# The opening of a transformer layer on one core: weight splits, second-half statistics and small vectors put in another order

## The chip, the cores and the metric

The kernel runs on one core of a Trainium2 chip. A core has TensorE (PE, matmuls), VectorE (DVE), ScalarE (ACT), GpSimd (POOL) and SyncE (SP, which here only issues DMAs), each with its own queue worked off in order, an on-chip memory of 128 partitions (SBUF) and accumulation banks (PSUM), and 16 DMA engines to HBM. The metric is the device time of one execution in microseconds (us); the number to predict is the median after the change.

## The reference

One encoder layer over 1024 tokens of width 1024: an input LayerNorm, one projection, three attention groups, an output projection, a second LayerNorm, a squared-ReLU feed-forward of width 4096 and a third LayerNorm.

```python
x = layer_norm(x, ln_in_g, ln_in_b)
proj = x @ w_in[l]
qa, ka, va, qb, kb, vb, qc, kc, vc = jnp.split(proj, split_points, axis=-1)
oa = neighbourhood_attention(...)      # 8x16 windows on a 16x64 grid, 4 heads
ob = sliding_window_gqa(...)           # +-128 tokens, sink logit per head, 8 heads
oc = differential_attention(...)       # p1 - lam * p2, 4 heads, RMS norm per head
mix = jnp.concatenate([oa, ob, oc], axis=-1) @ w_out[l]
x = layer_norm(alpha * x + mix, ln_mix_g[l], ln_mix_b[l])
hdn = jax.nn.relu(x @ w_ff1[l])
x = layer_norm(alpha * x + (hdn * hdn) @ w_ff2[l], ln_ff_g[l], ln_ff_b[l])
```

In the differential attention `lam = exp(sum(lq0*lk0)) - exp(sum(lq1*lk1)) + 0.2`, and the normed output is scaled by `diff_subln_g * 0.8`.

## The kernel before

Every float32 operand of a matmul is split into a high part (rounded to the type fp32r that TensorE takes) and a low part (the rest), and each product is three matmuls: high by high, high by low, low by high (`mm3`, line 138). A weight block is split by a cast and a subtraction.

The opening goes like this. Four token tiles of 128x1024 are loaded (`load_x(range(4))`, line 180), then constants, the first weights of the queries and keys of the differential attention (`first_w`, line 333, called for QC and KC), the other four tiles, the value weights (`load_vc`, line 373) and the norm's rows. `ln_half` (line 223) does four tiles at a time: `ln_stats` on VectorE (L208 statistics, L215 aggregate, L217 add epsilon), a power on GpSimd (L218), then the normalisation in place, on ScalarE (L234) or, for the second and fourth tile of the first half, on VectorE (L228). Then for each of eight feature blocks four PE transposes into one PSUM bank (L239), an eviction with gain and offset on ScalarE (L241), the cast to the high part on VectorE or ScalarE (L246, L244) and the subtraction for the low part on VectorE (L247). The transposes of the first tile run over the five banks that are free, then those of the second tile, and so on, so a bank is complete when the fourth tile is.

`first_w` casts the weight on VectorE (L338) and subtracts on GpSimd (L339). `feat_pieces` (line 342) does 24 matmuls for a half (`mm_feat`, line 328) and evicts them. `t5_vectors` (line 271) makes the relative-bias vectors with a few matmuls, `split_vc` (line 379) casts the value weights on ScalarE and subtracts on VectorE (L130 through `sub`), `vc(t)` does 24 matmuls of 256 columns for one token tile. `ln_rows_out` (line 253) writes the scaled norm as rows to HBM: two products with alpha and, for each tile, a product and a sum on GpSimd (L260), in place, so behind the tile's transposes. `scalars` (line 308) loads the lambda, sink and sub-norm vectors through SP's queue and works on them with small instructions; its place is behind the second half's features.

The order of the instructions on each engine is not the program's: with `schedule_with_timeline_sim` a planner sets it before the run, from its own estimates of times, with the program's order as priority. `tc.issue_after(ins)` adds for the instructions in its block an edge of order behind `ins`, for those on the engine of `ins` alone, with no semaphore. The 36 buffers of `page` hold tiles, features and weights.

## Time and profile before

| | |
|---|---|
| median of 3 runs | 1190.77 us (1190.58 to 1192.29) |
| profiled execution, its own time | 1192.13 us |
| its span from first to last instruction | 1190.4 us, mean granted TensorE clock 0.99 |
| busy, PE / VectorE / ScalarE / GpSimd | 1141.3 / 953.1 / 642.1 / 414.6 us |
| the chain that ended last | PE 79% of the span, VectorE 5%, ScalarE 3% |

The engines' busy shares are means over stages: projections and attention up to about 600 us, the feed-forward behind it. L12 is line 12 of the kernel before. In a timeline a line is one instruction or several of one kind (x2), with its start, its length, what it writes and reads, and in brackets the engine's idle time ahead of it with what ended that. Matmuls overlap, so the distance from one start to the next is what one costs.

### The profile page before, as it was taken

To read this page: it belongs to the slowest core of one execution; us is meant where nothing else is said; L and a number is where in the kernel's file an instruction comes from. 1 tells how busy PE (TensorE), PEld (TensorE's weight loads), DVE (VectorE), ACT (ScalarE), POOL (GpSimd) and SP (SyncE) were. 2 spreads that over 40 slices of the span, in tenths; PEclk is the share of its full clock that TensorE was granted. 3 is DMA by queue.
4 is the path that set the end of the run, shared out by engine and by line. 5 is a ranking of instruction groups with operands and counts; after the bars stand their busy time and mean duration, and the time that the engine had idled before them with its cause. 6 is when DMAs were issued, how large, how long until landed. Compare 5 with 4: busy or idle time off the path is not lost.

```text
span 1190.4 us, 17144 instructions
## 1 busy us (share of the span) xinstructions
PE 1141.3 (96%) x5642; PEld 947.8 (80%) x5642; DVE 953.1 (80%) x1858; ACT 642.1 (54%) x1253; POOL 414.6 (35%) x368
## 2 busy tenths in 40 slices
PE   3999999999998989998999999999999999999996
PEld 2788889878877878876788888888888888888885
DVE  7566899998656688976779998999774988787985
ACT  4435666666556887765664544445553444444530
POOL 3875666685665775430121222222210000000201
PEclk9999999999989989999999999999999999999998
DMA  8566845362878971214376687766599754355731
GB/s 278 154 237 207 263 143 172 113 171 89 264 212 239 223 168 54 89 71 125 117 237 211 226 277 264 258 246 233 185 333 348 225 197 163 115 164 181 232 122 71
DMA packets 139408, 228.46 MB, mean 192 GB/s; under 512 B 11884, under 2 KB 76300, under 8 KB 139320
## 3 DMA queue, kind: packets, MB, share of 16 engines
q1 hardware_dynamic: 123800, 178.60, 47.7%
q0 software_dynamic: 15520, 48.77, 11.9%
q8 instruction: 45, 0.74, 0.3%
q14 instruction: 43, 0.35, 0.1%
HBM read 157.54 MB, written 77.60 MB: 198 GB/s over the span
## 4 chain that ended last, share of the span: by engine, by line
PE 79%; DVE 5%; ACT 3%; issue 2%; POOL 0%; DMA 0%; SPq 0%; DVEq 0%; ACTq 0%; POOLq 0%
PE psm L144 15%; PE psS L967 11%; PE psS L1097 11%; PE pst L967 7%; PE psm L967 7%; PE pst L1097 5%; PE psm L1097 5%; PE pspv L1097 4%; PE pspv L515 2%; PE psS L471 2%; PE pst L500 2%; PE pspv L754 1%; DVE pg L130 1%; PE pspv L652 1%; PE psS L725 1%
## 5 line engine op out<-in xcount | busy, mean ns | idle before, releaser
L144 PE MATMUL psm<-pg,whi 128*128 128x512 f32 x448 | 153.5, 408 | 2.1 <-DVE pg L246 1.8
L218 POOL TENSOR_TENSOR bnve<-bnve,pw 128x1 f32<-128x1 f32 x24 | 22.5, 940 | 360.7 <-DVE bnve L217 357.5
L1097 PE MATMUL psS<-pg,pg 128*128 128x512 f32 x576 | 140.5, 389 | 0.0
L967 PE MATMUL psS<-pg,pg 128*128 128x512 f32 x576 | 136.2, 393 | 2.4 <-ACT pg L827 2.4
L967 PEld LDWEIGHTS psS<-pg,pg 128*128 128x128 f32 x576 | 108.6, 189 | 25.2 <-ACT pg L827 2.9
L1097 PEld LDWEIGHTS psS<-pg,pg 128*128 128x128 f32 x576 | 108.1, 188 | 22.4
L827 ACT CAST pg<-hr 128x512 fp32r<-128x512 f32 x112 | 69.3, 619 | 95.3 <-PE pst L1097 40.8
L144 PEld LDWEIGHTS psm<-pg,whi 128*128 128x128 f32 x448 | 84.2, 192 | 22.0 <-DVE pg L246 2.2
L478 ACT ACTIVATE pg<-pg,cst 128x1024 f32<-128x1024 f32 x64 | 73.9, 1154 | 51.4 <-DVE cst L474 48.4
L144 PE MATMUL psm<-pg,wlo 128*128 128x512 f32 x224 | 89.7, 401 | 0.8 <-POOL wlo L161 0.8
L967 PE MATMUL psm<-pg,pg 128*128 128x512 f32 x384 | 89.8, 389 | 0.0
L967 PE MATMUL pst<-pg,pg 128*128 128x512 f32 x384 | 89.6, 389 | 0.0
L828 DVE TENSOR_TENSOR pg<-hr,pg 128x512 fp32r<-128x512 f32 x112 | 76.7, 685 | 13.0 <-ACT pg L827 12.9
L967 PEld LDWEIGHTS psm<-pg,pg 128*128 128x128 f32 x384 | 72.1, 188 | 15.0
L967 PEld LDWEIGHTS pst<-pg,pg 128*128 128x128 f32 x384 | 72.1, 188 | 15.0
L130 DVE TENSOR_TENSOR pg<-pst,pg 128x512 fp32r<-128x512 f32 (+2 forms) x112 | 64.9, 589 | 22.6 <-ACT pg L640 8.4
L485 POOL TENSOR_TENSOR pg<-pg,cst 128x704 f32<-128x704 f32 x32 | 49.2, 1537 | 80.1 <-DVE cst L482 52.7
L1097 PE MATMUL pst<-pg,pg 128*128 128x512 f32 x288 | 74.2, 389 | 0.0
L1097 PE MATMUL psm<-pg,pg 128*128 128x512 f32 x288 | 74.2, 389 | 0.0
L975 POOL DMA_DIRECT2D hd<-evb x80 | 43.2, 541 | 86.4 <-DVE evb L823 82.0
L144 PE MATMUL psm<-whi,pg 128*128 128x256 f32 (+1 forms) x256 | 71.5, 346 | 0.8 <-DVE pg L130 0.5
L827 ACT CAST pg<-evb 128x512 fp32r<-128x512 f32 x80 | 48.6, 617 | 39.5 <-DVE evb L823 39.4
(208 smaller groups left out, 2758.8 us busy)
## 6 DMA issues: line engine op xcount, KB each, us to landing
hr<-hd SPq DMA_DIRECT2D x28, 1024.0 KB, 5.7
hd<-evb POOLq DMA_DIRECT2D x80, 256.0 KB, 3.8
w1r<-in_w_ff SPq DMA_DIRECT2D x16, 1024.0 KB
evb<-in_w_ff SPq DMA_DIRECT2D x64, 256.0 KB, 3.7
qk<-evb SPq DMA_DIRECT2D x52, 256.0 KB, 3.9
y<-pg POOLq DMA_DIRECT2D x24, 512.0 KB, 4.4
pg<-y SPq DMA_DIRECT2D x24, 512.0 KB, 5.5
pg<-in_w_ff SPq DMA_DIRECT2D x32, 256.0 KB, 7.8
```

What stands on the lines that cost most here:

```text
L130: nc.vector.tensor_tensor(out=o, in0=a, in1=b, op=ALU.subtract)
L144: mm = nc.tensor.matmul(o, a, b, start=(i == 0), stop=(i == n - 1))
L471: last_mm[0] = nc.tensor.matmul(sc, q[:, m, (i % 2) * P:(i % 2) * P + P], kst[h][kh][:, m, :], start=True, stop=True)
L478: nc.scalar.activation(out=rt, in_=rt, func=AF.Exp, scale=-1.0, bias=sm[:, m:m + 1], accum_out=sm[:, 2 + m:3 + m])
L485: nc.gpsimd.tensor_tensor(out=R[1][:, a], in0=R[1][:, a], in1=sm[:, 6:7].broadcast_to([P, C_POOL]), op=ALU.mult)
L500: nc.tensor.transpose(pt[:, kb * P:(kb + 1) * P], src[:, c0:c0 + P], ident)
L515: nc.tensor.matmul(pv[:, 0:256], Vc[h // 2][kb // 4][:, kb % 4, h % 2, :], src[:, kb % 4, :], start=(n == 0), stop=(n == 15))
L827: nc.scalar.copy(out=pg[:, 0], in_=x)
L828: last_split[0] = nc.vector.tensor_tensor(out=pg[:, 1], in0=x, in1=f32(pg[:, 0]), op=ALU.subtract)
L967: nc.tensor.matmul(o, w[:, e, k], xo[m][k][:, f], start=(n == 0), stop=(n == 11))
L975: nc.gpsimd.dma_start(out=hd_d[m - 1, j], in_=x)
L1097: nc.tensor.matmul(o, h[:, e, sl], w[:, f], start=(k == 0 and n == 0), stop=(k == 15 and n == 2))
```

## The change

Seven edits, all in the opening:

- `first_w` falls into `first_load` and `first_split`. The casts of the first two weights go behind the last VectorE normalisation of the first half (`last_norm`), their subtractions on GpSimd behind that half's last power (`last_pow`).
- `ln_half` falls into `ln_norm` and `ln_feats`. The second half's statistics on VectorE go behind the subtraction of the first half's seventh feature (`dc < 7` instead of `dc < 5`); before, only the normalisation had such a rule, of no effect on ScalarE.
- With these first weights `mm_feat` does the 16 products of the high weights first, then the eight of the low ones.
- `split_vc` subtracts on GpSimd instead of VectorE, behind the first weights' subtractions, and comes ahead of `t5_vectors`.
- The rows on GpSimd come behind these subtractions (`last_pool`).
- The small vectors are loaded by five DMAs from ScalarE's queue ahead of all others of the opening; `scalars` comes behind the first half's last VectorE normalisation, the difference for lambda goes to GpSimd behind the value weights and its offset to ScalarE (`lam_sum`).
- The value weights are loaded ahead of the second four token tiles.

```diff
--- before.py
+++ after.py
@@ -178,6 +178,36 @@
             xs.append(x_t)
     load_x(range(4))
+    lq = const([P, 2, 32], "lq")
+    lk = const([P, 2, 32], "lk")
+    lam = const([P, 4], "lam")
+    neglam = lam[:, 3:4]
+    g08 = const([P, 1], "g08")
+    sink = const([P, 8], "sink")
+    negsink = const([P, 8], "negsink")
+    nc.scalar.dma_start(out=lq, in_=bcast_row(A["diff_lam_q"], 64))
+    nc.scalar.dma_start(out=lk, in_=bcast_row(A["diff_lam_k"], 64))
+    for j in range(2):
+        nc.scalar.dma_start(out=g08[64 * j:64 * j + 64, :], in_=A["diff_subln_g"])
+    nc.scalar.dma_start(out=sink, in_=bcast_row(A["sw_sink"], 8))
+    def scalars():
+        nc.vector.tensor_tensor(out=lq, in0=lq, in1=lk, op=ALU.mult)
+        nc.vector.tensor_reduce(out=lam[:, 0:2], in_=lq, op=ALU.add, axis=AX.X)
+        nc.scalar.activation(out=lam[:, 0:2], in_=lam[:, 0:2], func=AF.Exp)
+        nc.vector.tensor_scalar(out=g08, in0=g08, scalar1=1.0 - LAM_INIT, scalar2=None, op0=ALU.mult)
+        nc.vector.tensor_scalar(out=negsink, in0=sink, scalar1=-1.0, scalar2=None, op0=ALU.mult)
+    def lam_sum():
+        with tc.issue_after(last_pool[0].ins):
+            nc.gpsimd.tensor_tensor(out=lam[:, 2:3], in0=lam[:, 1:2], in1=lam[:, 0:1], op=ALU.subtract)
+        nc.scalar.activation(out=lam[:, 3:4], in_=lam[:, 2:3], func=AF.Identity, bias=lam0)
+    lam0 = const([P, 1], "lam0")
+    nc.vector.memset(lam0, -LAM_INIT)
     ident = const([P, P], "ident")
     load(out=ident, in_=A["c_ident"])
     pw = const([P, 16], "pw")
@@ -220,18 +250,21 @@
     last_sub = [None]
-    def ln_half(xs, half, cols):
+    def ln_norm(xs, half):
         for j in range(4):
-            mean, rstd = ln_stats(xs[j])
+            with (tc.issue_after(last_sub[0].ins) if half else ExitStack()):
+                mean, rstd = ln_stats(xs[j])
             if half == 0 and j % 2:
-                nc.vector.tensor_scalar(out=xs[j], in0=xs[j], scalar1=mean, scalar2=rstd,
-                                        op0=ALU.subtract, op1=ALU.mult)
+                last_norm[0] = nc.vector.tensor_scalar(out=xs[j], in0=xs[j], scalar1=mean, scalar2=rstd,
+                                                       op0=ALU.subtract, op1=ALU.mult)
                 continue
             nmr = small([P, 1], "nmr", 2)
             nc.vector.scalar_tensor_tensor(out=nmr, in0=mean, scalar=-1.0, in1=rstd, op0=ALU.mult, op1=ALU.mult)
-            with (tc.issue_after(last_sub[0].ins) if half else ExitStack()):
-                nc.scalar.activation(out=xs[j], in_=xs[j], func=AF.Identity, scale=rstd, bias=nmr)
+            nc.scalar.activation(out=xs[j], in_=xs[j], func=AF.Identity, scale=rstd, bias=nmr)
+    def ln_feats(xs, half, cols):
         res = []
         for dc in range(8):
             pt = ps_t() if dc % 2 else ps_s()
@@ -245,14 +278,16 @@
             else:
                 nc.vector.tensor_copy(out=xp[:, 0, :], in_=pt)
             lo = nc.vector.tensor_tensor(out=xp[:, 1, :], in0=pt, in1=f32(xp[:, 0, :]), op=ALU.subtract)
-            if dc < 5:
+            if dc < 7:
                 last_sub[0] = lo
             res.append(xp)
         return res
+    last_norm = [None]
     def ln_rows_out(xs, rows, ydram):
-        with tc.issue_after(last_pow[0].ins):
+        with tc.issue_after(last_pool[0].ins), tc.issue_after(last_pow[0].ins):
             for r in rows:
                 nc.gpsimd.tensor_tensor(out=r, in0=r, in1=alpha.broadcast_to([P, D]), op=ALU.mult)
         for t in range(NT):
@@ -297,56 +332,49 @@
...
     w_in = A["w_in"]
     qk_d = {c0: dram([2, n, S], f"qk{c0}")
             for c0, n in ((QA, 256), (KA, 256), (QB, 512), (KB, 128), (QC, 256), (KC, 256))}
-    def mm_feat(w, half):
+    def mm_feat(w, half, lo_last=False):
         pm = ps_mm()
+        if lo_last:
+            seq = [(0, e, k) for k in range(8) for e in (0, 1)] + [(1, 0, k) for k in range(8)]
+            for n, (d, e, k) in enumerate(seq):
+                nc.tensor.matmul(pm, w[d][:, k, :], xT[half][k][:, e, :], start=(n == 0), stop=(n == 23))
+            return pm
         mm3(pm, [(w[0][:, k, :], w[1][:, k, :], xT[half][k][:, 0, :], xT[half][k][:, 1, :]) for k in range(8)])
         return pm
-    def first_w(base):
+    def first_load(base):
         raw = page([P, 8, P])
         load(out=raw, in_=w_cols(w_in, base, P))
-        hi = sb.tile([P, 8, P], F32R, tag="whi", bufs=2, name=nm("whi"))
-        lo = sb.tile([P, 8, P], F32R, tag="wlo", bufs=2, name=nm("wlo"))
-        nc.vector.tensor_copy(out=hi, in_=raw)
-        nc.gpsimd.tensor_tensor(out=lo, in0=raw, in1=f32(hi), op=ALU.subtract)
-        return hi, lo
+        return raw
+    def first_split(raws):
+        ws = []
+        for raw in raws:
+            hi = sb.tile([P, 8, P], F32R, tag="whi", bufs=2, name=nm("whi"))
+            with tc.issue_after(last_norm[0].ins):
+                nc.vector.tensor_copy(out=hi, in_=raw)
+            ws.append((hi, sb.tile([P, 8, P], F32R, tag="wlo", bufs=2, name=nm("wlo"))))
+        for raw, (hi, lo) in zip(raws, ws):
+            with tc.issue_after(last_pow[0].ins):
+                last_pool[0] = nc.gpsimd.tensor_tensor(out=lo, in0=raw, in1=f32(hi), op=ALU.subtract)
+        return ws
+    last_pool = [None]
     def feat_pieces(base, f, scale, banded=False, w=None, pool=True):
+        first = w is not None
         w = list(w or ())
         def piece(half):
             if not w:
                 w.extend(split_w(w_cols(w_in, base + f * P, P), [P, 8, P], pool=pool))
-            pm = mm_feat(w, half)
+            pm = mm_feat(w, half, first)
             eh = evb([P, 512], F32R)
             el = evb([P, 512], F32R)
             if banded:
@@ -381,7 +409,8 @@
         for raw in raws:
             hi, lo = page([P, 4, 256], F32R), page([P, 4, 256], F32R)
             nc.scalar.copy(out=hi, in_=raw)
-            sub(lo, raw, f32(hi))
+            with tc.issue_after(last_pool[0].ins):
+                last_pool[0] = nc.gpsimd.tensor_tensor(out=lo, in0=raw, in1=f32(hi), op=ALU.subtract)
             w.append((hi, lo))
         return w
@@ -1107,16 +1136,22 @@
     cols_in = ln_load("ln_in")
-    qc = feat_pieces(QC, 0, CSC, w=first_w(QC))
-    kc = feat_pieces(KC, 0, 1.0, w=first_w(KC))
+    first_raws = [first_load(QC), first_load(KC)]
+    raws_vc = load_vc()
     load_x(range(4, NT))
-    raws_vc = load_vc()
     rows_in = ln_rows("ln_in")
-    xT[0] = ln_half(xs[0:4], 0, cols_in)
+    ln_norm(xs[0:4], 0)
+    with tc.issue_after(last_norm[0].ins):
+        scalars()
+    first_ws = first_split(first_raws)
+    qc = feat_pieces(QC, 0, CSC, w=first_ws[0])
+    kc = feat_pieces(KC, 0, 1.0, w=first_ws[1])
+    xT[0] = ln_feats(xs[0:4], 0, cols_in)
     qc[0]()
     kc[0]()
+    wv = split_vc(raws_vc)
+    lam_sum()
     t5_vectors()
-    wv = split_vc(raws_vc)
     def vc(t):
         if t % 4 == 0:
@@ -1126,12 +1161,11 @@
     for t in range(4):
         vc(t)
-    xT[1] = ln_half(xs[4:8], 1, cols_in)
+    ln_norm(xs[4:8], 1)
+    xT[1] = ln_feats(xs[4:8], 1, cols_in)
     ln_rows_out(xs, rows_in, y1)
     qc[1]()
     kc[1]()
-    with tc.issue_after(last_sub[0].ins):
-        scalars()
     tabs_c[0] = toeplitz_c(0)
     for t in range(4, NT):
         vc(t)
```

## Rows read from the trace of the kernel before

**Rows 1.** Stretches: length, busy time (instructions) of each engine, granted clock, DMA

```profile
30.10:44.30 14.20, 14.20 (x52) 7.68 (x51) 10.59 (x9) 8.93 (x13) 14.20 (x7) 1.00 0.08 27
...
57.70:87.00 29.30, 28.36 (x177) 24.55 (x176) 16.76 (x28) 10.96 (x22) 21.93 (x10) 1.00 0.67 234
...
87.00:330.00 243.00, 240.42 (x1383) 204.10 (x1382) 209.09 (x507) 152.17 (x275) 152.18 (x95) 1.00 0.58 179
...
600.00:1180.00 580.00, 580.00 (x2561) 480.25 (x2560) 485.27 (x775) 264.92 (x464) 77.02 (x129) 1.00 0.63 217
```

**Rows 2.** PE's order of time, 15 to 51 us

```profile
15.00 0.42 PE L239 MATMUL psS<-ident,pg 128*128 128x128 f32 x1
...
18.86 0.47 PE L239 MATMUL psS<-ident,pg 128*128 128x128 f32 x1 [3.44 <-DVE pg L228]
...
22.04 1.22 PE L144 MATMUL psm<-pg,whi 128*128 128x512 f32 x2 [1.85 <-DVE pg L246]
...
24.72 1.08 PE L239 MATMUL psS<-ident,pg 128*128 128x128 f32 x4 [1.46 <-DVE pg L247]
...
29.44 0.63 PE L144 MATMUL psm<-pg,wlo 128*128 128x512 f32 x1
...
29.86 0.74 PE L144 MATMUL psm<-pg,whi 128*128 128x512 f32 x2
...
30.45 0.40 PE L144 MATMUL psm<-pg,wlo 128*128 128x512 f32 x1
...
30.68 0.39 PE L144 MATMUL psm<-pg,whi 128*128 128x512 f32 x1
...
44.31 6.02 PE L144 MATMUL pst<-pg,pg 128*128 128x256 f32 x48
```

**Rows 3.** VectorE's order of time, 11 to 42 us

```profile
11.05 0.80 DVE L228 TENSOR_SCALAR pg<-pg,bnmv,bnve 128x1024 f32<-128x1024 f32 x1
...
11.89 0.65 DVE L338 CAST whi<-pg 128x1024 fp32r<-128x1024 f32 x1
...
12.68 0.15 DVE L217 TENSOR_SCALAR bnve<-bnmv 128x1 f32<-128x1 f32 x1
...
13.54 2.01 DVE L338 CAST whi<-pg 128x1024 fp32r<-128x1024 f32 x1 [0.71 <-DMA pg<-in_w_in]
...
16.66 2.15 DVE L228 TENSOR_SCALAR pg<-pg,bnmv,bnve 128x1024 f32<-128x1024 f32 x1
...
20.05 1.27 DVE L208 BATCH_NORM_STATS2 bnst<-pg 128x6 f32<-128x512 f32 x2
...
21.36 0.63 DVE L246 CAST pg<-psS 128x512 fp32r<-128x512 f32 x1
...
34.96 6.35 DVE L130 TENSOR_TENSOR pg<-pg,pg 128x1024 fp32r<-128x1024 f32 x2
```

**Rows 4.** GpSimd's order of time, 9 to 87 us

```profile
9.72 0.56 POOL L218 TENSOR_TENSOR bnve<-bnve,pw 128x1 f32<-128x1 f32 x1 [1.88 <-DVE nmr L232]
...
12.61 2.38 POOL L339 TENSOR_TENSOR wlo<-pg,whi 128x1024 fp32r<-128x1024 f32 x1
...
14.96 0.99 POOL L218 TENSOR_TENSOR bnve<-bnve,pw 128x1 f32<-128x1 f32 x1
...
65.07 20.89 POOL L260 TENSOR_TENSOR pg<-pg,pg 128x1024 f32<-128x1024 f32 x8 [9.88 <-PE pst L239]
```

**Rows 5.** ScalarE's order of time, first evictions and casts

```profile
19.38 0.75 ACT L241 ACTIVATE psS<-psS,ln_in_cols 128x512 f32<-128x512 f32 x1 [5.34 <-PE psS L239]
...
22.71 1.10 ACT L244 CAST pg<-pst 128x512 fp32r<-128x512 f32 x2
```

**Rows 6.** Stretches of the loads; last columns: DMA share, GB/s

```profile
1.70:8.20 6.50, 0.00 (x0) 0.00 (x0) 2.89 (x7) 0.52 (x2) 0.56 (x1) 1.00 0.96 330
...
22.30:24.50 2.20, 0.96 (x2) 0.24 (x2) 2.20 (x7) 2.20 (x4) 0.39 (x1) 1.00 0.86 149
```

**Rows 7.** A stretch at a lower granted clock (PEclk, third column from the end)

```profile
347.50:354.40 6.90, 5.95 (x22) 5.50 (x23) 4.04 (x11) 2.53 (x7) 4.03 (x2) 0.51 0.69 199
```

20 lines of the change are left out of this document (removed).

## Prediction

> **What bounds the kernel now.** I read the windows by stage first. From 600 to 1180 us PE is busy for all of its 580 us, and from 87 to 330 us for 240.42 of 243 [rows 1]. The feed-forward part is bound by PE alone, so time can come only from stretches in which PE waits. The next view is PE's own order of time [rows 2]: between the third token tile's last transpose (15.00) and the fourth tile's first (18.86) PE waits 3.44 us for VectorE's normalisation (L228). The first real matmul comes at 22.04. After it PE waits another 1.46 us, runs without a gap from 24.72, and still needs 0.42 us from one 512-column matmul to the next at 29.44; from 30.45 it needs 0.23. [...] From 30.10 PE is full (14.20 of 14.20 us) [rows 1]. So the opening ends on PE, and what it starts late is lost for good.
>
> Why late? VectorE's and GpSimd's orders of time tell it [rows 3, 4]. The fourth tile's variance is ready at 12.83 (12.68 plus 0.15). Its power on GpSimd should then take 0.56 (the row at 9.72), but GpSimd began the first weight's low part (L339, 2.38 us) at 12.61, so the power starts at 14.96 and takes 0.99. The normalisation that follows (16.66) runs beside the second weight's low part, which comes behind that power, and takes 2.15 us, where the same instruction took 0.80 alone at 11.05. The weight cast shows the same pair: 0.65 alone, 2.01 beside GpSimd. Then VectorE works on a statistic of the second half (20.05, 1.27 us) before it casts the first feature (21.36).
>
> **The change, part by part.** *Weights behind the first norm.* The two casts go behind the fourth tile's normalisation on VectorE, the two low parts behind its power on GpSimd. The power then runs from 12.8 to 13.4, the normalisation to 14.2, against 18.81 (16.66 plus 2.15). PE is busy with the third tile until 15.2, so the last transposes start there and not at 18.86: 3.65 us gained. ScalarE's first eviction began 0.52 us behind that transpose (19.38) and takes 0.75 [rows 5]: now 15.7 to 16.5. VectorE has, from 14.2, four small instructions of the lambda and sink vectors (about 0.15 to 0.2 each, by the 128x1 row at 12.68: 0.7) and two casts of 0.65, so it is free at 16.2. The feature cast starts at 16.5 and the first matmul, which stood 0.68 us behind its start, at 17.2: 4.9 us earlier. If the second cast meets GpSimd's first low part, it takes 2.01 instead of 0.65, VectorE is free only at 17.6, and 3.8 us remain. I take the short end, since that cast stands right behind the first in VectorE's queue, while GpSimd must first see the first one end.
>
> *Low products last.* The low weights are ready at about 18 and 20.4 (15.6 for the first cast's end, then 2.4 us each); the 16 matmuls that read them stand behind the other 32, so PE doesn't wait for them. This costs nothing; in the old order PE would meet both within its first matmuls and wait up to 3 us.
>
> *Statistics behind the first features.* Before, four statistics of 1.27 us each, and the four normalisations of the second half on ScalarE, lie among the first half's evictions. Behind the change the eight features cost VectorE four casts and eight subtractions (12 of about 0.65 by the row at 21.36, 7.9 us) and ScalarE eight evictions of 0.75 and four casts of 0.55 (8.2 us, [rows 5]): one feature per 1.05 us. [...] Gain of this part 1.5 us. [...] The postponed work, some 7 us on VectorE from about 24 and four normalisations, ends near 33 to 36. Until then PE has the rest of the query and key matmuls and the bias vectors, and then four token tiles of values, which took 6.02 us for two from 44.31 on [rows 2]; from some 38 us on they last till 50. That is more than ten us of cover. Without it each microsecond would count in full.
>
> *Values' low parts from VectorE to GpSimd.* VectorE loses two instructions of together 6.35 us (34.96, beside GpSimd's rows) [rows 3]; GpSimd gains two of 2.4 us, ahead of its rows, and the tiny lambda difference. The rows' second half starts only when PE has transposed that half (65.07, after 9.88 us idle) [rows 4]: 5 us fit. Neither side is on PE's path; I put 0. [...]
>
> *Vectors earlier, five small DMAs on ScalarE's queue.* They leave SP's queue, where nothing critical stood behind them, and ScalarE is idle until its first normalisation, so their issue is free. But the token tiles fill the DMA engines from 1.7 to 8.2 us at a share of 0.96 [rows 6], and the third tile is waited for. The trace doesn't show these five among the tiles. Bounds: 0, and 1.9 us (the stretch 22.3 to 24.5 in which they run before, 2.2 us at 0.86, other transfers in it). I take 0.4, near zero, because they carry 68 KB and a tile 512. [...]
>
> *New waits.* The statistics' VectorE instruction that follows the power now waits for GpSimd behind the weights' and values' low parts (four of 2.4 us); behind it on VectorE stand the last feature's subtraction and the first evictions, for which PE waits. Bounds 0 to 4.8 (two low parts); I take 0, because the planner orders the queues by such times.
>
> Sum: 4.9 - 0.4 + 1.5 = 6.0 us. The profiled execution took 1192.1 (span 1190.4), 1.4 above the median of the three runs; it would become 1186.1, the span 1184.4, and the median **1184.8**.
>
> **The rivals.** [...] 0.15.
>
> *Smaller gain:* the second cast loses to GpSimd (1.1), the small DMAs delay the third tile (1.5 more than put), or VectorE stands behind GpSimd's power; two of these leave about 3: 1187.8. For it: the 2.01 and 2.15 us rows. 0.20.
>
> *No gain to measure:* the start is early, but attention doesn't begin earlier, because its scores need keys and bias tables over a chain of stores and loads through HBM, or the queues were put in another order than meant and the subtractions still stand first. Then 1190 to 1191. Against it: 57.7 to 87 has PE busy for 28.36 of 29.30 us [rows 1], so little of that chain is bare. 0.13.
>
> *Slower:* the program's order on each engine is planned anew from the changed opening. Later PE runs at half clock after gaps; one such fall, 347.5 to 354.4, is 6.9 us at 0.51 [rows 7], so 3.4 us lost, with a gap of one to three us ahead of it. Two falls more cost some 10.5 and outweigh 6.0: 1195.3. One alone doesn't turn the sign; two decide. 0.10.
>
> **How the numbers follow.** My forecast, 4.5 to 8 us gained, gets 0.42. With the larger and the smaller gain, faster by over 0.2% (2.4 us, about what a measurement of this kernel can tell from no change) has 0.77, within it 0.13, slower 0.10. The range reaches from 1179.5 (9.0 and half a fall of the clock saved) to 1190.5; what lies outside is the slower case, half of "no gain" and a little below, together under 2 in 10.
>
> **What would show it.** Right: the fourth tile's normalisation takes 0.8 us and ends near 14.2; the first 512-column matmul starts near 17; no wait for the low weights; matmuls at 0.23 us spacing from about 23; the value matmuls begin near 38 instead of 44.3. Wrong: the third tile's statistics later than 8.3, a cast of 2 us ahead of the first feature, VectorE idle behind a power around 24 to 30, or more stretches at half clock between 330 and 600.

## The result, and the profile after it

| | before | after |
|---|---|---|
| median | 1192.65 us (1190.58 to 1195.41, 10 runs) | 1201.24 us (1193.35 to 1207.59, 10 runs) |
| profiled execution, its span | 1192.13, 1190.4 us | 1207.59, 1205.8 us |

The ratio is 1.0069 (95% interval 1.0049 to 1.0088): 0.7% slower, where 0.5% faster was forecast. The changed kernel's runs also lie 14 us apart, those of the kernel before 5. The profiled run is the longest of the ten.

The opening came as forecast. PE's order of time in the changed kernel (L272 transposes, L344 the first weights' matmuls, L314 the bias vectors):

```profile
15.11 0.69 PE L272 MATMUL psS<-ident,pg 128*128 128x128 f32 x2 [1.73 <-ACT pg L264]
...
17.37 1.22 PE L344 MATMUL psm<-pg,whi 128*128 128x512 f32 x2
...
19.02 1.18 PE L344 MATMUL psm<-pg,whi 128*128 128x512 f32 x4
...
27.91 2.30 PE L314 MATMUL psS<-onehot,t 32*4 32x512 f32 x5 [0.91 <-DMA t<-in_t_table]
```

The first 512-column matmul starts at 17.37 instead of 22.04 [rows 2], four of them take 1.18 us at 19.02 already, and the last value matmul of the first half starts at 49.9 instead of 57.6: 7.7 us ahead. These are the last 24 of them, in the changed kernel and in the kernel before:

```profile
47.15 3.03 PE L144 MATMUL pst<-pg,pg 128*128 128x256 f32 x24
```

```profile
54.83 3.04 PE L144 MATMUL pst<-pg,pg 128*128 128x256 f32 x24
```

VectorE's order of time shows how (L259 normalisation, L360 weight casts, L279 feature cast):

```profile
6.40 1.28 DVE L238 BATCH_NORM_STATS2 bnst<-pg 128x6 f32<-128x512 f32 x2 [5.41 <-DMA pg<-in_x]
...
14.14 0.81 DVE L259 TENSOR_SCALAR pg<-pg,bnmv,bnve 128x1024 f32<-128x1024 f32 x1 [0.36 <-POOL bnve L248]
...
15.14 1.29 DVE L360 CAST whi<-pg 128x1024 fp32r<-128x1024 f32 x2
...
16.62 0.69 DVE L279 CAST pg<-psS 128x512 fp32r<-128x512 f32 x1
```

The 2.01 and 2.15 us of [rows 3] are 0.65 each (two casts in 1.29) and 0.81. Then the lead is lost. The windows of the changed kernel, columns as in [rows 1]:

```profile
57.70:87.00 29.30, 20.46 (x111) 17.88 (x109) 16.03 (x8) 4.30 (x8) 20.52 (x13) 0.83 0.64 216
87.00:330.00 243.00, 234.69 (x1338) 198.19 (x1339) 199.71 (x496) 147.30 (x265) 140.84 (x85) 0.99 0.54 163
330.00:460.00 130.00, 116.55 (x657) 97.83 (x656) 82.47 (x217) 88.39 (x229) 88.43 (x68) 0.97 0.85 215
...
600.00:1180.00 580.00, 578.55 (x2547) 478.85 (x2548) 488.57 (x781) 278.82 (x488) 74.14 (x129) 1.00 0.64 218
```

From 57.7 to 87 PE is busy for 20.46 us where it was 28.36, and VectorE has 8 instructions for 28. One of them lasts 13 us. VectorE's, then GpSimd's, then PE's order of time in that stretch (L161 is the subtraction that makes a background weight's low part, `split_w`; L295 and L296 are GpSimd's rows and their stores, L260 and L261 before):

```profile
58.05 0.69 DVE L280 TENSOR_TENSOR pg<-pst,pg 128x512 fp32r<-128x512 f32 x1 [0.28 <-ACT pg L277]
64.22 13.02 DVE L161 TENSOR_TENSOR wlo<-raw,whi 128x1024 fp32r<-128x1024 f32 x1 [5.47 <-PE psm L344]
77.16 0.68 DVE L391 SCALAR_TENSOR_TENSOR evb<-psm,evb 128x512 fp32r<-128x512 f32 x1
...
86.44 1.22 DVE L161 TENSOR_TENSOR wlo<-raw,whi 128x1024 fp32r<-128x1024 f32 x1 [7.18 <-ACT whi L159]
```

```profile
56.79 9.48 POOL L295 TENSOR_TENSOR pg<-pg,pg 128x1024 f32<-128x1024 f32 x4
66.23 0.58 POOL L296 DMA_DIRECT2D y<-pg  x1
66.83 9.31 POOL L295 TENSOR_TENSOR pg<-pg,pg 128x1024 f32<-128x1024 f32 x4
76.09 2.16 POOL L296 DMA_DIRECT2D y<-pg  x4
```

```profile
66.06 4.23 PE L144 MATMUL pst<-pg,pg 128*128 128x256 f32 x34
77.89 1.22 PE L144 MATMUL psm<-pg,whi 128*128 128x512 f32 x2 [7.60 <-DVE evb L391]
...
88.64 3.11 PE L144 MATMUL pst<-pg,pg 128*128 128x256 f32 x24 [2.87 <-DVE pg L130]
91.58 0.40 PE L500 MATMUL psS<-pg,ev 128*128 128x512 f32 x1
```

The subtraction takes 13.02 us; the next one, alone, takes 1.22. It ends at 77.24, 1.1 us behind the last row (76.14): it came in only when the rows were through, and five of the eight row instructions ran meanwhile. Behind it in VectorE's queue stand the evictions L391 and L130, so PE waits 7.60 us and comes back at half clock (granted clock 0.50 from 77.5 to 80.0 us, 0.83 in the window). The weight's buffer comes free late too: there is one `raw`, the second weight's load is issued only at 77.27, and ScalarE's cast of it, ahead of evictions in ScalarE's queue, waits for it:

```profile
85.36 1.05 ACT L159 CAST whi<-raw 128x1024 fp32r<-128x1024 f32 x1 [6.42 <-DMA raw<-in_w_in]
```

That is PE's 2.87 us at 88.64. The first score matmul of the differential attention starts at 91.58 instead of 87.00, so 12.3 us are lost between 50 and 92. The kernel before has it here:

```profile
87.00 0.85 PE L471 MATMUL psS<-pg,ev 128*128 128x512 f32 x3
```

In the kernel before the same two subtractions met the rows as well [rows 4]:

```profile
72.90 2.74 DVE L161 TENSOR_TENSOR wlo<-raw,whi 128x1024 fp32r<-128x1024 f32 x1 [4.60 <-ACT whi L159]
80.88 2.83 DVE L161 TENSOR_TENSOR wlo<-raw,whi 128x1024 fp32r<-128x1024 f32 x1 [2.75 <-ACT whi L159]
```

The changed kernel's profile ends 15.4 us behind that of the kernel before (1205.8 and 1190.4), and only 4.6 of them are there at the first score. From it to the first matmul of the feed-forward the changed kernel takes 487.1 us and the kernel before 476.7, so 10.3 more are lost in the attention; from there to the end the two differ by 0.5. The feed-forward's first matmuls, changed kernel and kernel before:

```profile
578.65 1.09 PE L996 MATMUL psS<-pg,pg 128*128 128x512 f32 x4
```

```profile
563.72 1.09 PE L967 MATMUL psS<-pg,pg 128*128 128x512 f32 x4
```

### The profile page after: what moved, and what is told of

It reads as the page before. It is cut to its first block, busy times and chain, and to the rows that moved or that the text cites. A ratio compares the mean times of both kernels' runs of the same rounds, so it can differ in the third digit from the quotient of the medians.

```text
span 1205.8 us, 17142 instructions
## 1 busy us (share of the span) xinstructions
PE 1144.0 (95%) x5642; PEld 948.6 (79%) x5642; DVE 947.9 (79%) x1855; ACT 643.0 (53%) x1254; POOL 412.2 (34%) x371
## 4 chain that ended last, share of the span: by engine, by line
PE 82%; DMA 8%; DVE 4%; ACT 3%; issue 2%; SPq 0%; POOL 0%; DVEq 0%; POOLq 0%; ACTq 0%
PE psm L144 17%; PE psS L1126 11%; PE psS L996 11%; PE pst L996 7%; PE psm L996 7%; PE pst L1126 5%; PE psm L1126 5%; PE pspv L1126 4%; DMA pg<-qk 2%; PE pspv L544 2%; PE psS L500 2%; PE pst L529 2%; DMA qk<-evb 1%; PE pspv L783 1%; PE psm L344 1%
## 5 line engine op out<-in xcount | busy, mean ns | idle before, releaser
L144 PE MATMUL psm<-pg,whi 128*128 128x512 f32 x384 | 130.5, 408 | 7.6 <-DVE evb L391 7.6
L144 PEld LDWEIGHTS psm<-pg,whi 128*128 128x128 f32 x384 | 72.8, 193 | 23.2 <-DVE evb L391 7.8
L130 DVE TENSOR_TENSOR pg<-pst,pg 128x512 fp32r<-128x512 f32 (+2 forms) x112 | 65.3, 590 | 30.4 <-ACT pg L669 9.1
L144 PE MATMUL psm<-pg,wlo 128*128 128x512 f32 x192 | 77.8, 405 | 0.0
```

What stands on the lines that cost most here:

```text
L130: nc.vector.tensor_tensor(out=o, in0=a, in1=b, op=ALU.subtract)
L144: mm = nc.tensor.matmul(o, a, b, start=(i == 0), stop=(i == n - 1))
```

## Experiments

Theory A: VectorE's two-input subtraction is held by GpSimd's run of rows, for a length that differs from run to run. Theory B: the order planned anew costs the time. C (late weights through the one `raw` buffer) and D (the bias table's load) came up on the way.

| kernel | median us | ratio to before (95%) |
|---|---|---|
| after_again | 1200.93 | 1.0065 (1.0035 to 1.0095) |
| after_no_rows | 1183.61 | 0.9915 (0.9881 to 0.9949) |
| before_no_rows | 1204.37 | 1.0089 (1.0063 to 1.0116) |
| after_pool_split | 1197.00 | 1.0041 (1.0017 to 1.0066) |
| after_rows_wait | 1199.29 | 1.0070 (1.0042 to 1.0098) |
| after_raw2 | 1195.31 | 1.0022 (0.9997 to 1.0047) |
| after_t5_early | 1208.50 | 1.0135 (1.0117 to 1.0152) |
| after_vectors_back | 1207.32 | 1.0129 (1.0112 to 1.0145) |
| after_gap | 1187.31 | 0.9951 (0.9936 to 0.9966) |
| after_gap_raw2 | 1188.87 | 0.9956 (0.9941 to 0.9971) |
| after_vec_sp | 1210.28 | 1.0154 (1.0135 to 1.0174) |
| after_gap_raw2_vec | 1186.60 | 0.9939 (0.9926 to 0.9952) |
| before_gap | 1196.79 | 1.0022 (1.0009 to 1.0035) |
| after_gap_mid | 1185.28 | 0.9929 (0.9915 to 0.9942) |
| after_gap_mid_norm | 1180.38 | 0.9887 (0.9873 to 0.9901) |
| before_gap_norm | 1196.76 | 1.0027 (1.0017 to 1.0037) |

**after_again**, the changed kernel once more.

> The changed kernel as it is. In its first profile one VectorE subtraction (L161, the low part of the first background weight, two SBUF inputs) took 13.02 us beside GpSimd's rows of the second half, where the kernel before took 2.74 for the same one. Theory A (VectorE waits for GpSimd's run of rows, for a length that changes from run to run): the runs spread by over 8 us again, and in this profile the span is near 1205.8 less what L161 falls short of 13.02. Theory B (the new order of the instructions costs the time, whatever L161 does): the span stays near 1200 to 1206 even if L161 takes about 3 us.

1193.86 to 1210.13 in eleven runs, and 1213.1 in one that the ratio leaves out, so the spread is its own. This profile (span 1195.5) has no long hold; the two subtractions on VectorE:

```profile
70.36 2.80 DVE L161 TENSOR_TENSOR wlo<-raw,whi 128x1024 fp32r<-128x1024 f32 x1 [5.45 <-PE psm L344]
...
78.84 2.38 DVE L161 TENSOR_TENSOR wlo<-raw,whi 128x1024 fp32r<-128x1024 f32 x1 [3.65 <-ACT whi L159]
```

Theory A had the span at 1205.8 less 10.2, so 1195.6, and theory B at 1200 to 1206. That A's number came so near is partly luck, because this profile loses elsewhere: PE's wait for the bias table (PE's order of time) is followed by a stretch at half clock (a window; granted clock 0.54).

```profile
27.79 3.65 PE L314 MATMUL psS<-onehot,t 32*4 32x512 f32 x6 [0.98 <-DMA t<-in_t_table]
```

```profile
30.10:44.30 14.20, 14.20 (x36) 8.19 (x35) 4.52 (x6) 6.83 (x9) 14.20 (x11) 0.54 0.29 95
```

PE does 36 matmuls there where the profile of the result has 88. The first score is 1.9 us ahead of before, and the span ends 5.1 behind: from that score to the feed-forward it takes 483.4 us, the kernel before 476.7. So this execution, without a long hold, is no faster than the kernel before either. The hold, then, is not all.

**after_no_rows and before_no_rows.**

```diff
-            for k, op in enumerate((ALU.mult, ALU.add)):
+            for k, op in enumerate((ALU.mult, ALU.add)) if t < 4 else ():
```

> The changed kernel without the products and sums of the second half's four row tiles (they go to HBM as normalised). This leaves out eight GpSimd instructions of 2.4 us, so nothing runs beside the background weight's subtraction. Theory A: L161 takes about 1.2 us, the opening's lead of some 8 us stays, the time is 1182 to 1188 and the runs agree within 3 us. Theory B: 1195 or more.

> The control: the kernel before, without the same eight GpSimd instructions. Theory A and theory B: L161 goes from 2.74 to about 1.2 us, the time stays within 0.3% of the kernel before (1187 to 1195), since VectorE got in after one row there.

The changed kernel without the rows gained 17.3 us on after_again and had no hold; its four runs still lie 10 us apart (1177.93 to 1187.97), where A expected 3. The control broke both expectations: the kernel before got slower. Its profile says why; the new order put the value weights' subtraction (L130) beside the rows of the first half. VectorE's and GpSimd's order of time:

```profile
33.75 19.79 DVE L130 TENSOR_TENSOR pg<-pg,pg 128x1024 fp32r<-128x1024 f32 x2
```

```profile
39.76 11.55 POOL L260 TENSOR_TENSOR pg<-pg,pg 128x1024 f32<-128x1024 f32 x5
```

Two instructions in 19.79 us, the first of them 18.65; [rows 3] had the two in 6.35. So the hold is no property of the change: another order that put such an instruction beside the rows had it too.

**after_pool_split**: L161 of the two background weights on GpSimd, behind the rows.

```diff
-    add_bg(5.2, feat_pieces(QC, 1, CSC, pool=False))
-    add_bg(5.2, feat_pieces(KC, 1, 1.0, pool=False))
+    add_bg(5.2, feat_pieces(QC, 1, CSC))
+    add_bg(5.2, feat_pieces(KC, 1, 1.0))
```

> The changed kernel, whole, but the low parts of the first two background weights are subtracted on GpSimd, in its own queue among the rows, instead of on VectorE. Theory A: no VectorE instruction with two SBUF inputs meets the rows, the evictions behind it on VectorE go on, the time is 1184 to 1190 and the runs agree within 3 us. Theory B: 1195 or more. A third case: PE waits for GpSimd, which comes to the low part only behind some rows; then 1189 to 1194 with a PE wait for L161 on GpSimd.

No hold, first score 11.6 us ahead of before, but 8.9 us of ScalarE's wait for a `raw` load at 262 us, PE's wait behind it and 10.2 us at half clock; end +3.6. The median, 1197.0, misses A's 1184 to 1190 and meets B's 1195 or more: with the hold gone, the lead was lost in the attention, which took 491.8 us from the first score to the feed-forward. This made theory C.

**after_rows_wait**: the rows of tiles 4 to 7 written behind the background weights in the program.

```diff
+                with (tc.issue_after(wait.ins) if wait and k == 0 else ExitStack()):   # wait: L161 on VectorE
+                    nc.gpsimd.tensor_tensor(out=xs[t], in0=xs[t], in1=rows[k], op=op)
```

> The changed kernel whole, with one wait more: GpSimd's rows of tiles 4 and 5 begin behind VectorE's low part of the first background weight, those of tiles 6 and 7 behind that of the second, so that both subtractions find GpSimd idle. Theory A (VectorE's subtraction held beside GpSimd's rows costs the lead): both subtractions at L161 take 1.2 to 1.6 us instead of 2.4 to 13.0, the first C scores come 5 to 8 us before the kernel before instead of 1.9 to 4.6 behind it, and if nothing else is lost the median is 1183 to 1188. Theory C (the lead is given back behind it, in the stage of the differential attention, by weights that come late through the one raw buffer, whatever the rows do): the subtractions are short all the same, the lead is there at the first C scores, and most of it is gone by the last C transposition; median 1193 to 1199, as with the low parts on GpSimd (1197.0).

My mistake: `issue_after` orders instructions of one engine and puts no semaphore. The rows ran from 61.04, the subtraction came at 68.82 beside them (2.79 us). It is a repeat of the changed kernel in another order and no test of the wait. Like after_again it has no long hold in its profile and is still slower than the kernel before.

**after_raw2**

```diff
-N_PG = 36
+N_PG = 35
...
-            raw = sb.tile(shape, F32, tag="raw", bufs=1, name=nm("raw"))
+            raw = sb.tile(shape, F32, tag="raw", bufs=2, name=nm("raw"))
```

> The changed kernel whole, with two raw buffers for the background weights instead of one, and 35 pages instead of 36 to make room: the second weight can be loaded before the first is split. Theory C: the waits of ScalarE's cast L159 for a raw load (6.1 to 8.9 us in the changed kernel and its variants) fall under 2 us, PE's stall between 120 and 140 us shrinks from 4 to under 2, and the kernel is 4 to 8 us faster than the changed one: 1193 to 1197; a hold at L161 may still come and is then worth its 1 to 10 us. Theory A alone: the raw buffer changes nothing that decides, the hold beside the rows stays, and the median stays at 1198 to 1204. The page that is missing could cost by itself: a wait for a page in the differential stage would show it.

5.9 us faster than the changed kernel at the medians, although its profile has a hold of 13.06 us; ScalarE's waits for `raw` loads up to 150 us are gone (12.5 us in the profile of the result). From the first score to the feed-forward it takes 478.2 us instead of 487.1, and behind that 4.3 more than the changed kernel. So theory C has a part in the loss, some 9 us of that stage in these two profiles; by the times its size is not sure, as the intervals of this run and of after_again overlap.

**after_t5_early**: the table's two loads in a function of their own, called earlier.

```diff
...
+    t5_load()
     load_x(range(4, NT))
```

> The changed kernel whole, with the loads of the one-hot table and of the t5 table issued ahead of the token tiles 4 to 7 and of the rows. PE's wait at 26.5 to 27.9 us in front of the bias vectors (0.91 and 0.98 us in two runs, in one of them followed by 13.7 us at half clock) goes. Theory D (this gap and the clock behind it are part of the loss): no half-clock stretch before 57 us, last value matmul of the first half at 49 to 50 in each profile, and the spread of the changed kernel's runs (1193 to 1213) shrinks from above; median 1196 to 1199. If the gap is only a companion, the median stays at 1200 to 1202. The order behind the opening is planned anew by this edit as by the change, so 3 us either way can come from that.

The wait at 27 us went, theory D's gain didn't come: the profile has a hold of 14.57 us, and all four runs are at 1206 to 1210. With that hold in it the run can't tell what the wait alone costs.

**after_vectors_back**: `scalars` with its loads and `sub` as in the kernel before, `lam_sum` gone.

```diff
...
     kc[1]()
+    with tc.issue_after(last_sub[0].ins):
+        scalars()
```

> The changed kernel without its part on the small vectors: lambda, gain and sink vectors are loaded on SP and worked on by VectorE behind the second half's features, as in the kernel before; the rest of the change stays. Measures the price of the five small loads beside the token tiles: the first statistic should come back from 6.40 to about 4.5 us, the first 512-column matmul from 17.37 to about 15.5, and the last value matmul of the first half from 49.9 to 48. If the opening alone set the time, the median would be 1.9 under the changed kernel, 1199.3. Theory A and C: what is lost lies behind 57 us and is not touched, 1196 to 1203; the rows still run beside the low part L161, and a hold of 2 to 13 us there is to be seen again.

The first matmul came at 15.50, as expected, so the five small loads cost 1.87 us. But now the vectors' first product met the rows:

```profile
55.32 19.09 DVE L194 TENSOR_TENSOR lq<-lq,lk 128x64 f32<-128x64 f32 x1
```

64 columns, 19.09 us, up to the end of the rows at 74.27; ahead of the rows the same product takes 0.22. All four runs are at 1206.7 to 1207.9. In the changed order it is the vectors' early place that keeps this product away from the rows.

**after_gap**, a true wait. Half of the rows stand behind an instruction of GpSimd that reads VectorE's result:

```diff
...
+            v = f32(lo[:, 0, 0:1])
+            with tc.issue_after(last_row[0].ins):
+                gate = nc.gpsimd.tensor_tensor(out=dep[:, n:n + 1], in0=v, in1=v, op=ALU.subtract)
+        for t in ts:            # tiles 4, 5 behind the first weight, 6, 7 behind the second
```

> The changed kernel whole, with a true wait in GpSimd's queue: a 128x1 subtraction of GpSimd reads the low part of the first background weight ahead of the rows of tiles 4 and 5, and a second one that of the second weight ahead of tiles 6 and 7. (The edge of after_rows_wait was one of order on one engine and held nothing back: its rows ran from 61.04, ahead of VectorE's subtraction at 68.82.) GpSimd stands still until VectorE is through. Theory A: both subtractions take 1.2 to 1.4 us; no DVE instruction over 3 us before 100 us; first C scores 6 to 8 us before the kernel before; runs close together, none above 1200; median 1186 to 1194, that is 7 or more below the changed kernel (1201). Theory C on top of it: 3 to 6 us of the lead are lost again between 120 and 145 us, so 1190 to 1196 rather than 1185. Theory B (the new order costs the time, the hold only shows beside it): median 1198 or more.

1184.71 to 1190.95: 13.9 us under the changed kernel, 5.8 under the kernel before (0.49%, 4.1 to 7.6 us by the interval). GpSimd waits, VectorE doesn't, and PE is full in the window (lines behind L161 are shifted by the edit):

```profile
68.59 0.19 POOL L304 TENSOR_TENSOR dep<-wlo 128x1 f32<-128x1 f32 x1 [11.46 <-DVE wlo L161]
```

```profile
67.28 1.23 DVE L161 TENSOR_TENSOR wlo<-raw,whi 128x1024 fp32r<-128x1024 f32 x1 [5.36 <-PE psm L357]
...
74.03 2.93 DVE L161 TENSOR_TENSOR wlo<-raw,whi 128x1024 fp32r<-128x1024 f32 x1 [2.34 <-ACT whi L159]
```

```profile
57.70:87.00 29.30, 29.30 (x178) 26.07 (x177) 14.47 (x27) 9.67 (x19) 18.39 (x11) 1.00 0.74 237
```

The second subtraction still met the first half of the gated rows, for one instruction. PE's first score comes 6.0 us ahead of before, and theory B's 1198 or more did not come:

```profile
80.97 0.87 PE L513 MATMUL psS<-pg,ev 128*128 128x512 f32 x3
```

**before_gap**, the same wait in the kernel before.

> The kernel before with the true wait of after_gap in GpSimd's queue ahead of the rows of tiles 4 and 5, and of 6 and 7; nothing of the change. It says what the wait is worth without the change. Its subtractions at L161 took 2.74 and 2.83 us, 1.5 each over 1.23, so by theory A the wait can bring 1 to 3 us here and no more: 1189 to 1193, and the change under the wait (after_gap, 1187.3) is then worth 2 to 6 us. By theory B the wait itself plans a better order and helps here as much as there: 1180 to 1184.

It gains nothing: 1196.79, 0.2% slower than before, and the interval leaves out equal. The first score is 1.8 us earlier, and the order behind it, planned anew, gives back more: the feed-forward starts 5.5 us later than before. So the wait is not a gain by itself, and theory B holds in this much: an edit that plans the order anew moves the later stages, here by 7.3 us between the first score and the feed-forward.

**after_gap_raw2, after_vec_sp, after_gap_raw2_vec.** The first is after_gap with the edit of after_raw2. The second has no wait of GpSimd, but the five loads on SP (diff) and `scalars` behind the first features. The third has all.

```diff
...
     raws_vc = load_vc()
+    vec_load()              # lq, lk, g08 twice, sink, by load() instead of nc.scalar.dma_start
     load_x(range(4, NT))
```

> after_gap with two raw buffers for the background weights and 35 pages instead of 36. Theories A and C together: no hold at L161, the raw loads of the differential stage come a weight earlier, ScalarE's casts L159 wait for them under 2 us, the lead at the first C scores (6 to 8) is still at least 4 at the last C transposition; median 1183 to 1189, faster than the kernel before. If C is wrong (the late loads aren't what costs the lead), it is no better than after_gap, within 2 us of it.

> The changed kernel with the five small loads on SP's queue behind the weights, ahead of token tiles 4 to 7, and the vectors worked on behind the first features, still ahead of GpSimd's rows. First statistic at 4.2 to 4.5 us instead of 6.40, first 512-column matmul at 15.5 instead of 17.37, and no VectorE work of the vectors beside the rows, where after_vectors_back had one 128x64 product held for 19.09 us. If the time of the opening counts in full, 1.9 us under the changed kernel; but the hold at L161 can come as before, so with theory A the runs spread as those of the changed kernel, 1192 to 1208, median 1197 to 1203.

> All three together: GpSimd's true wait, two raw buffers, the small loads on SP behind the weights. If the three prices add up, the opening is 1.9 us earlier than in after_gap_raw2, no hold, no late raw loads: median 1181 to 1187, 6 to 11 us under the kernel before. Each edit plans the order behind it anew; if that alone decides by some 5 us either way, as theory B has it, it lands anywhere from 1183 to 1197.

Without a hold the second `raw` buffer brings nothing in the time (1188.87 against 1187.31), as C's counter-case said, but not because late loads are free. From the first score to the feed-forward after_gap_raw2 takes 474.1 us, after_gap 481.5; the gain is given back behind it. The three kernels with this edit (two `raw` buffers, 35 pages) take 631.1, 631.5 and 635.2 us from the feed-forward's first matmul to the end, all others 625.9 to 627.2. The missing page is the likely cause, though no run has it alone: in after_gap_raw2_vec PE waits 3.3 us in the second feed-forward matmul, where the kernel before has no such wait. From PE's waits (total, times, longest), then from its order of time:

```profile
PE psS L1141 <- ACT pg L871: 3.3, 1, 3.3
```

```profile
19.27 1.09 PE L278 MATMUL psS<-ident,pg 128*128 128x128 f32 x4 [2.92 <-DVE lam L205]
```

The second line shows the vectors' new place: a 128x8 instruction of theirs beside GpSimd's first low part took 2.14 us instead of 0.16, and PE waited 2.92. after_vec_sp had that and a hold of 13.99: 1210.28.

**after_gap_mid and after_gap_mid_norm.** The five loads on SP between the norm's columns and the first weights; then also a third wait, GpSimd's scaling behind the second half's last `nmr`:

```diff
...
+    vec_load()
     first_raws = [first_load(QC), first_load(KC)]
...
+            v = last_nmr[0]
+                gate = nc.gpsimd.tensor_tensor(out=dep[:, 2:3], in0=v, in1=v, op=ALU.subtract)
```

> after_gap with the five small loads on SP's queue between the columns of the norm and the first weights, and the vectors worked on where the change has them. First statistic at 4.2 to 4.5 us instead of 6.40, weights 0.5 to 1 us later, first 512-column matmul at 15.5 to 16 instead of 17.37, without the 2.92 us wait for a small vector instruction that after_gap_raw2_vec had at 16.3 to 19.3. If the opening counts: 1185 to 1186, one to two under after_gap; if later gaps and clock falls take it, within 1 us of after_gap (1187.3).

> after_gap_mid with a third true wait in GpSimd's queue, ahead of the scaling of the two rows: it reads the last 128x1 vector of the second half's normalisation. In after_gap two of these vectors took 1.77 and 2.43 us on VectorE beside the scaling, where two others took 0.16, and PE ran at half clock from 29.1 for 6.8 us. Expected: all four at 0.16, the second half's normalisation on ScalarE 3 to 4 us earlier, no half-clock stretch between 25 and 57 us, and 2 to 4 us less than after_gap_mid. If PE has other work there anyway, no difference over 1 us.

The first gave 2.0 us, as much as expected but not in the way expected: the statistic comes at 4.46, but the loads now delay the weights, the second cast waits 1.08 us for its own and meets GpSimd (1.92), and the first matmul is at 17.93. The second gave 4.9 more. `nmr` on VectorE in after_gap_mid, then in after_gap_mid_norm, and the latter's window:

```profile
34.11 1.86 DVE L269 SCALAR_TENSOR_TENSOR nmr<-bnmv,bnve 128x1 f32<-128x1 f32 x1 [0.85 <-POOL bnve L254]
```

```profile
34.81 0.16 DVE L269 SCALAR_TENSOR_TENSOR nmr<-bnmv,bnve 128x1 f32<-128x1 f32 x1 [0.86 <-POOL bnve L254]
```

```profile
330.00:460.00 130.00, 121.34 (x683) 100.98 (x682) 96.05 (x249) 98.68 (x259) 89.71 (x69) 1.00 0.78 191
```

The small vectors are quick, as expected, but the 4.9 us are not theirs: at the first score after_gap_mid leads by 8.7, this one by 6.6. They come behind 330 us, where the granted clock stays at 1.00; in the kernel before it fell there three times up to 600 us (0.51, 0.50 and 0.52 in the windows of the falls), for 6.8, 6.8 and 3.4 us, half of which, 8.5 us of work, is lost by my estimate. This profile has no fall ahead of the last microseconds. That is luck of the order, or a gain that I can't derive.

**before_gap_norm**, the same three waits in the kernel before.

> The kernel before with the three true waits of after_gap_mid_norm in GpSimd's queue: ahead of the scaling, of the rows of tiles 4 and 5, of 6 and 7; nothing of the change. before_gap was 1196.8 with two of them. If the third wait earns by itself what it earned on the changed kernel (4.9 us, 1185.3 to 1180.4), this one is at 1190 to 1193, and the change with cheaper small loads is worth 10 to 12 us under equal waits. If the waits are no help to the kernel before, whose first row instruction of GpSimd begins at 28.5 us beside statistics, 1194 to 1198.

1196.76: no gain. By the ratios 1.0027 and 0.9887, the change (with its small loads on SP) is worth 1.4%, 16.4 us by the medians, under equal waits, of which only the lead at the first score (6.6 against 1.8, so 4.8) is its own in a way that the traces follow. The rest lies between that score and the feed-forward, 471.4 us against 484.6, with no half clock there against 23.9 us of it.

**The 18 profiles of the layer side by side.** Six have a hold of 13 us or more, and these executions took 1202.5 to 1210.3 us; none of the twelve others took over 1199.3. So the hold goes with the long executions. It does not explain the others of the changed kernel, which are no faster than before. From the first score to the feed-forward the profiles take 471.4 to 491.8 us. Four have at most 3.4 us at half clock in that stretch and take 471.4 to 474.1; the other fourteen have 6.8 to 23.9 and take 476.7 to 491.8. Whether the half clock makes the stretch long, or the waits that come with it, no run separates.

**hold_alone**, the pair by itself. It sets two forms of theory A against each other. A1: VectorE comes in at the next boundary between two instructions of GpSimd, so no subtraction takes over 1.2 + 2.4 = 3.6 us, and beside 128x512 ones under 2.4. A2: it can be passed over at boundary after boundary, so some take 10 to 17 us and end with GpSimd's eighth product, the 128x64 product among them. By both, casts and the subtraction from PSUM stay under 1.5 us.

```python
prev = nc.gpsimd.tensor_tensor(out=x[k][:, c:c + width], in0=x[k][:, c:c + width], in1=g[:, c:c + width], op=ALU.mult)
...
d = nc.vector.tensor_copy(out=pd, in_=first[:, D - 512:D])      # released by the first product
d = nc.vector.tensor_copy(out=pd, in_=pd)                       # ticks - 1 times
...
nc.vector.tensor_tensor(out=lo, in0=raw, in1=f32(hi), op=ALU.subtract)
```

> None of the layer is computed: only the disputed pair of instructions, 43 times. GpSimd does eight 128x1024 products in place, back to back; VectorE is released by the first of them, copies 1 to 5 times 128x512 to PSUM to vary its place within GpSimd's instruction, and then does one operation: the 128x1024 subtraction of two SBUF tiles (as L161), a 128x64 product of two SBUF tiles, a 128x1024 cast of one, or a 128x512 subtraction of PSUM and SBUF; in some GpSimd issues a store after the fourth product, and in the last five its instructions are 128x512. [...]

VectorE's order of time; L107 is the 128x1024 subtraction, L110 the 128x64 product, L116 the one from PSUM. The last two lines stand beside GpSimd's 128x512 instructions:

```profile
38.99 2.74 DVE L107 TENSOR_TENSOR lo<-raw,hi 128x1024 fp32r<-128x1024 f32 x1
...
137.31 1.74 DVE L110 TENSOR_TENSOR small<-raw,hi 128x64 f32<-128x64 f32 x1
...
269.72 0.68 DVE L116 TENSOR_TENSOR lo<-pm,hi 128x512 fp32r<-128x512 f32 x1
...
776.61 1.66 DVE L107 TENSOR_TENSOR lo<-raw,hi 128x1024 fp32r<-128x1024 f32 x1
797.99 16.80 DVE L107 TENSOR_TENSOR lo<-raw,hi 128x1024 fp32r<-128x1024 f32 x1
```

Beside 128x1024 instructions A1 holds in all cases: VectorE gets in at the next boundary (the subtraction takes 1.27 to 2.84 us), and the GpSimd instruction that then waits takes 3.32 instead of 2.34. Beside 128x512 ones two of five were held for 16.80 and 15.33, as A2 says. The subtraction from PSUM never waited (0.68); a cast did (1.48, 2.31, for 0.65 alone [rows 3]), against both theories.

**hold_phase**, 32 places within GpSimd's instruction.

> None of the layer is computed: 32 times the pair of hold_alone, with GpSimd's instructions as in the changed kernel (four 128x1024 products in place, then four sums on the same tiles) and VectorE's subtraction of two SBUF tiles begun at 32 different places of the second to fourth of them, some 0.08 us apart. In hold_alone no 128x1024 case was held for long, but none began in the first 0.58 us of an instruction of GpSimd; of the 128x512 cases the two held for 16.80 and 15.33 us began 0.18 and 0.43 us into one, the others 0.67 to 1.17. Theory P (the place decides: who comes in the first half microsecond is passed over until GpSimd pauses): the cases that begin within 0.5 us of an instruction's start take 10 us and more, all others at most 2.9. In the layer's kernels the place alone did not sort them (held: 0.10, 0.31, 0.34, but also 1.09, 1.61, 1.70). Theory Q (something else in the kernel decides, such as other traffic): no case of the 32 over 2.9 us.

```profile
335.52 1.28 DVE L107 TENSOR_TENSOR lo<-raw,hi 128x1024 fp32r<-128x1024 f32 x1
355.45 3.30 DVE L107 TENSOR_TENSOR lo<-raw,hi 128x1024 fp32r<-128x1024 f32 x1
```

From 3.30 (0.11 us into the instruction) down to 1.28 (2.15 into it), without an exception: always the next boundary. Beside 128x1024 instructions the place does not make the long hold, and theory P falls there; six cases lie over Q's bound of 2.9 us, by at most 0.4. Beside 128x512 instructions, where the two held cases began 0.18 and 0.43 us into one, it was not tried.

## Why the prediction was wrong

*The opening* (4.9) was right in sum, 17.37 for 17.2, by two errors that cancel. The small DMAs were put at 0.4 with bounds 0 and 1.9; the first tile landed 1.9 later (6.40 for 4.47), the upper end, and after_vectors_back gives 1.87 for the first matmul. That they carry 68 KB against 512 was no reason for the low end. The chain behind them was shorter than I made it: without them (after_vectors_back) the first matmul is at 15.50, not at 17.2. My wrong sign "third tile's statistics later than 8.3" did show, at 9.47. The forecast's own row-based bound had it right.

*Statistics behind the first features* (1.5, the wait of 1.46 us ahead of 24.72 [rows 2]): the wait went. The 0.23 us spacing, forecast from about 23, stands at about 19 already, for 30.45 before [rows 2], and the lead at 49.9 us is 7.7, more than the sum's 6.0. The larger gain (0.15) and the range's lower end use 9.0 us, an estimate of mine that no run shows; the runs showed these 7.7, and they were lost by the first score. A wait of 0.91 to 0.98 us for the bias table came instead; in one profile, after_again's, the stretch at a granted clock of 0.54 follows it.

*Everything behind the opening, put at 0*, is the step that failed. "So little of that chain is bare" read PE's 28.36 of 29.30 us [rows 1] as cover. It showed that VectorE kept pace there in that run, with 2.74 and 2.83 us per subtraction; it did not show what one VectorE instruction more or less held would do, and PE had some 6 us in store (it stops at about 70.3, with VectorE in its hold since 64.22). In its place came one subtraction of 13.02 us, and 12.3 us were lost by the first score. The rows that could have told were in the prediction: 2.01, 2.15 and 6.35 us beside GpSimd [rows 3], each priced as a meeting with one GpSimd instruction. I asked which meetings the change removes, not which it leaves: eight row instructions of the second half beside two subtractions that stand ahead of evictions. That a meeting can last to the end of the run, the rows of before did not show; it should have been a rival with a price, at most 8 x 2.4 less what PE has in store.

The same 0 stood for the attention behind the first score, and there the new order cost 10.3 us in the profile of the result and 6.7 in that of after_again, which has no long hold. Late weights through the one `raw` buffer and stretches at half clock go with it (after_raw2, the 18 profiles); which of them is the cause stays open. The forecast had this only in its slower rival.

*Values' low parts at 0* stands: no wait of PE leads there. So do *Low products last* and *New waits*: PE doesn't wait for the low weights and is full from 30.10 to 44.30, although VectorE idles 1.43 us behind a power up to 30.95, one of the signs named as wrong.

*The slower rival* (two more falls of the clock, 1195.3, at 0.10) had the side right and the cause only in part. The changed profile has such falls at 73.6 and 138.4 us (granted clock 0.50), but the first follows the hold; without the hold and with the order planned anew (after_gap) the change comes out at 1187.3, 5.8 us under before, against the 6.0 of the sum. That the two agree is partly chance: after_gap had 6.8 us at half clock at 29 us and gave back some of a lead of 6.8 behind 300 us.

One number of the range is off: its lower end by its own terms is 1190.8 less 9.0 and 1.7, so 1180.1 and not 1179.5; nothing hangs on it.

The difference of after_gap and after, 13.9 us at the medians, is not theory A's part alone: of the 16.6 us between the two profiles 10.6 are there at the first score, behind the hold, and 5.6 come in the attention, whose order the edit moves as well. before_gap shows that the wait alone brings nothing. What remains open: why a hold ends at the next boundary in one execution and behind the run's last row in another of the same kernel; and why the half-clock falls behind 330 us come and go with the order.

## What to carry to other kernels

Before moving work, list for VectorE's two-input SBUF instructions which run of GpSimd instructions each will meet afterwards, and what stands behind it in VectorE's queue: the price to bound it by is the whole run, not one instruction (here 13.0 to 19.1 us, where a row takes 2.4). Where such a run has time to spare, let GpSimd wait through data for VectorE's result (an `issue_after` across engines held nothing: in after_rows_wait the rows ran from 61.04, the subtraction from 68.82), and test that wait on the old kernel as well, since there the wait and its new order made it 3.5 us slower. A busy engine in a profile says that its feeders kept pace in that run, not that they had slack.

## What the runs showed of the hardware that was not expected

- A VectorE instruction with two SBUF inputs took 13.0 to 19.1 us beside five to eight row instructions of GpSimd (13.02, 13.06, 13.99, 14.57, 18.65, 19.09) and ended behind the last of them, a 128x64 one as a 128x1024 one; GpSimd's stores between two groups of rows (66.23 to 66.83) did not end it. In hold_phase it came in at the next boundary in all 32 cases and took at most 3.30 us. The long holds go beyond that: VectorE's instruction had begun ahead of four to seven boundaries between rows and came in only behind the run's last row.
- Shorter GpSimd instructions did not help: the two long holds of hold_alone (16.80 and 15.33 us) stand beside the 128x512 ones.
- Tiny VectorE instructions waited too: the 128x1 product of two SBUF vectors (`nmr`) took 1.86 and 2.43 us, the 128x8 product of one SBUF vector and a constant (`negsink`) 2.14, for 0.16 each alone. One that reads PSUM and one SBUF tile did not (0.68, hold_alone).
